# Forgetting-attention scores from split float32r operands, in a hybrid decoder block on one core

## The chip, the cores and the metric

The kernel runs on one core of one Trainium2 chip. Its metric is device time in microseconds (us), from the start to the end of one execution. TensorE (PE in the profile) multiplies, VectorE (DVE) and ScalarE (ACT) do elementwise work, GpSimd (POOL) and SyncE (SP) mostly issue DMAs.

## The reference, cut to what matters

A decoder block over 272 tokens (16 meta tokens and 256 of the input), width 2048: one large projection feeds a gated DeltaNet branch and a forgetting-attention branch of 16 heads, both are gated and merged, and an MLP follows. The change lies in the scores of the attention branch.

```python
q = heads(rms_norm(q.reshape(B, L, FOX_HEADS, FOX_DH), q_norm_g))   # 16 heads of 128
k = heads(rms_norm(k.reshape(B, L, FOX_HEADS, FOX_DH), k_norm_g))
...
s = jnp.einsum('bhqd,bhkd->bhqk', qs, k).astype(jnp.float32) * scale
s = s + cq[..., :, None] - c[..., None, :]
s = jnp.where(kpos[None, :] <= qpos[:, None], s, -jnp.inf)
p = jax.nn.softmax(s, axis=-1).astype(v.dtype)
return jnp.einsum('bhqk,bhkd->bhqd', p, v)
```

Only the 256 input tokens are kept as queries (two tiles of 128); the first tile sees 144 keys, the second 272.

## The kernel before, in words

Weights stream from HBM in blocks of 1 MB. SP issues the loads, and `split` (L126) turns each half block into a high and a low float32r part: ACT copies it to `wh`, DVE subtracts to get `wl`. The pool `wspl` keeps three such pairs. A gemm with stationary weights (`gemm_ws`, L156) takes 16 steps of contraction, so two blocks and four splits; each step has three products (L168, L169, L170) for each of two column groups, 96 in all, into two PSUM banks (`acc`). The pool `psA` has four such banks, so a gemm takes the banks of the gemm two before it, and can start only when these have been read.

The stage around the change is the value projection of the attention branch: eight gemms, one for a pair of heads, called V0 to V7 here (L950). After each, two heads are put on a task list, an even and an odd one. A head is a generator (`fox_head`, L885): after every step of a gemm each head on the list is advanced to its next `yield`, so heads are recorded between the steps of later gemms. V0 to V7 are followed by four gemms on `C_Z` columns (`gemm_ts`, L971), called Z0 to Z3, recorded after all heads have ended.

A head does this: DVE reads its bank and scales it to `vt` (L888), which frees the bank; POOL issues a DMA that copies it to `vb`. PE makes the scores (L894 to L897) from `qf` and `kf`, with a masking product in bfloat16 for each tile; DVE scales them to `tl` (L902), finds the maxima `nm`, ACT takes exponentials, DVE divides by the sum; POOL issues a DMA `tl` to `tb`. PE transposes `vb` ("v flips") and `tb` with a small tile `pm` ("p flips"), both on L94; the results are split into high and low (`vnh`, `vnl`, `pth`, `ptl`, and `ptm` for the meta tokens); L939 to L944 are the products of probabilities and values, and `ybh`, `ybl` the result.

All temporary tiles of a head come from pools with a fixed number of buffers in rotation: `t272` (129 to 272 elements a partition) has 12, `t512` has 4. Before the change a head takes four of `t272`: `vt`, `vb`, `vnh`, `vnl`. The order of instructions on each engine is set when the program is built: a scheduler orders them by its own estimates, within what the pools allow, and each engine then runs its row strictly in that order.

Of the kernel before, what the change touches and what calls it, by code (L numbers as in the profile page):

```python
# [9 lines left out]
F32R = mybir.dt.float32r  # L10
BF16 = mybir.dt.bfloat16
AF = mybir.ActivationFunctionType
ALU = mybir.AluOpType
AX = mybir.AxisListType

P = 128
# [3 lines left out]
T = NM + 256  # L20
# [13 lines left out]
def hybrid_block(ctx: ExitStack, tc: tile.TileContext, x, meta_tokens, mix_norm_g, w_in, conv_w, a_log,  # L34
# [23 lines left out]
    def tt(shape, name, dtype=F32):  # L58
        n = 1
        for d in shape[1:]:  # L60
            n *= d
        for size, tag in ((128, "t128"), (272, "t272"), (512, "t512")):
            if n <= size:
                return tmp.tile(shape, dtype, name=name, tag=tag, bufs=TMP_BUFS[tag])
        raise ValueError(n)

    def big_tile(shape, name, dtype=F32):
        return big.tile(shape, dtype, name=name, tag="big")
# [4 lines left out]
    def ps_tile():  # L73
        return psS.tile([P, 512], F32, name="ps", tag="ps")

    def acc_tile():
        return psA.tile([P, 512], F32, name="acc", tag="acc")

    act, dve, pe, pool = nc.scalar, nc.vector, nc.tensor, nc.gpsimd

    def acopy(out, in_, scale=1.0):
        act.activation(out=out, in_=in_, func=AF.Copy, scale=scale)  # L82

    def f(ap):
        return ap.bitcast(F32)
# [11 lines left out]
    def stack(dst, src, both):  # L97
        n = list(src.shape)
        one = 1 if both == (0, 2) else 2
        acopy(dst[..., both[0]:both[1] + 1:both[1] - both[0], :], src.unsqueeze(len(n) - 1).broadcast_to(n[:-1] + [2, n[-1]]))  # L100
        dve.tensor_tensor(out=dst[..., one, :], in0=src, in1=f(dst[..., 0, :]), op=ALU.subtract)
# [20 lines left out]
    def pause(n):  # L122
        for _ in range(n):
            yield
# [96 lines left out]
    with tc.high_priority():  # L221
# [3 lines left out]
        for i in range(4):  # L225
            s = slice(i * 512, (i + 1) * 512)
# [14 lines left out]
    identb = const.tile([P, P], BF16, name="identb")  # L241
# [3 lines left out]
    maskb = const.tile([P, P], BF16, name="maskb")  # L245
# [10 lines left out]
    ps = acc_tile()  # L256
# [570 lines left out]
    kf = big_tile([P, H, T], "kf")  # L827
# [56 lines left out]
    rng = (slice(0, 144), slice(144, 416))  # L884
    def fox_head(h, acc):  # L885
        qf, rq = QF[h], RQ[:, h, :]
# [3 lines left out]
        vb = bits(vt[:, NM:T], [P, 256], "vb")  # L890
        vs = tt([P, 3, NM], "vs", F32R)
        stack(vs, vt[:, 0:NM], (0, 2))
        ps = ps_tile()
        pe.matmul(ps[:, 0:144], qf[:, 0:P], kf[:, h, 0:144], start=True, stop=False)  # L894
        pe.matmul(ps[:, 16:144], identb, maskb, start=False, stop=True)
        pe.matmul(ps[:, 144:416], qf[:, P:256], kf[:, h, :], start=True, stop=False)  # L896
        pe.matmul(ps[:, 288:416], identb, maskb, start=False, stop=True)  # L897
        tl = tt([P, 416], "tl")
        nm = tt([P, 2], "nm")
        su = tt([P, 2], "su")  # L900
        for t in range(2):
            dve.scalar_tensor_tensor(out=tl[:, rng[t]], in0=ps[:, rng[t]], scalar=rq[:, t:t + 1],  # L902
                                     in1=NC[:, h, 0:144 + 128 * t], op0=ALU.mult, op1=ALU.add)
# [4 lines left out]
        ps = ps_tile()  # L908
# [18 lines left out]
        ps, ps2 = ps_tile(), ps_tile()  # L927
# [10 lines left out]
        ps = ps_tile()  # L938
# [10 lines left out]
    for hp in range(H // 2):  # L949
        accs = gemm_ws(win, C_FV + hp * 256, u, 0, T)  # L950
        for c in range(2):
            tasks.append(fox_head(2 * hp + c, accs[c]))
# [17 lines left out]
    for n in range(4):  # L970
        accs = gemm_ts(win, C_Z + n * 512, u_t(0), u_t(1), KT)  # L971
        yy = []
        for t in range(2):
# [4 lines left out]
            for i in range(4):  # L978
                h = 4 * n + i
# [5 lines left out]
        for i in range(2):  # L985
            ps = ps_tile()
# [192 lines left out]
```

## Time and profile before

| | |
|---|---|
| median of 3 runs | 1989.97 us (1988.95 to 1992.73) |
| the profiled execution | 1992.09 us, span 1990.3 us |
| PE, DVE, ACT, POOL busy | 1966.9, 1200.4, 1008.2, 115.1 us |
| mean granted TensorE clock | 0.997 |
| value stage with its heads | about 616 to 770 us |

Busy time of an engine is the union of its instructions. A matmul's row shows how long it lies in the pipeline; what it costs in a stream is the distance from its start to the next start. The share of an engine over the whole span says little on one stage, so the stage is read by itself.

### The profile page before, as it was taken

The numbers are of one execution on the slowest core, as the hardware profiler recorded it, in microseconds if no ns is written. First come the engines' busy times: TensorE is split into PE (matmuls) and PEld (weight loads), VectorE is DVE, ScalarE is ACT, GpSimd is POOL, SyncE is SP. The second block draws the span as 40 slices with busy tenths as digits, with TensorE's granted clock in tenths as the row PEclk, the third lists the DMA queues.
The fourth block names the chain that finished last, engine by engine and source line by source line (L and its number), as shares of the span: only waits on it lengthen the run. The fifth ranks groups of instructions, "written<-read, shape, count | busy, mean of one in ns | idle before, by whom it ended". The sixth has DMA issues, their size and how long they took to land.

```text
span 1990.3 us, 30185 instructions
## 1 busy us (share of the span) xinstructions
PE 1966.9 (99%) x11974; PEld 1735.0 (87%) x11974; DVE 1200.4 (60%) x2005; ACT 1008.2 (51%) x1797; POOL 115.1 (6%) x168
## 2 busy tenths in 40 slices
PE   8999999999999999999999999999999999999998
PEld 7898999999999998888888888888888888888886
DVE  5786846677546776644444555566655456665555
ACT  5644466556555555444444445555543345554444
POOL 0022100011131110000000000000000000000000
PEclk9999999999999999999999999999999999999999
DMA  6556766544566545656565666666655566666555
GB/s 201 171 162 204 217 179 205 165 140 141 182 210 198 165 165 200 203 190 201 190 201 190 201 243 212 199 188 188 188 191 193 197 194 186 188 186 212 196 197 176
DMA packets 283139, 378.77 MB, mean 190 GB/s; under 512 B 24163, under 2 KB 190406, under 8 KB 282470
## 3 DMA queue, kind: packets, MB, share of 16 engines
q1 hardware_dynamic: 275584, 353.65, 56.3%
q0 software_dynamic: 7200, 22.92, 3.5%
q8 instruction: 94, 1.54, 0.3%
q14 instruction: 47, 0.39, 0.1%
q10 hardware_dynamic: 214, 0.28, 0.0%
HBM read 351.63 MB, written 3.76 MB: 179 GB/s over the span
## 4 chain that ended last, share of the span: by engine, by line
PE 93%; issue 3%; DMA 2%; DVE 1%; ACT 0%; SPq 0%; POOL 0%; POOLq 0%; DVEq 0%; ACTq 0%
PE acc L165 15%; PE acc L183 15%; PE acc L185 15%; PE acc L184 15%; PE acc L170 14%; PE acc L168 7%; PE acc L169 7%; PE ps L94 1%; DVE wl L131 1%; DMA kb<-kT 1%; PE ps L552 0%; DMA rawS<-in_w_in_dram 0%; PE ps L896 0%; PE ps L628 0%; DMA dY<-I 0%
## 5 line engine op out<-in xcount | busy, mean ns | idle before, releaser
L131 DVE TENSOR_TENSOR wl<-raw,wh 128x1024 fp32r<-128x1024 f32 x644 | 787.7, 1224 | 635.1 <-ACT wh L82 631.8
L82 ACT ACTIVATE wh<-raw 128x1024 fp32r<-128x1024 f32 x644 | 682.1, 1060 | 751.8 <-PE acc L185 463.7
L170 PE MATMUL acc<-u,wl 128*128 128x272 f32 (+2 forms) x1536 | 440.5, 290 | 0.6 <-DVE wl L131 0.6
L168 PE MATMUL acc<-u,wh 128*128 128x272 f32 (+1 forms) x1280 | 373.0, 293 | 1.0 <-DVE ca L465 1.0
L169 PE MATMUL acc<-u,wh 128*128 128x272 f32 (+1 forms) x1280 | 371.8, 291 | 0.0
L165 PE MATMUL acc<-v,wh 128*128 128x512 f32 x1024 | 355.8, 396 | 0.0
L170 PEld LDWEIGHTS acc<-u,wl 128*128 128x128 f32 x1536 | 289.6, 189 | 3.2 <-DVE wl L131 1.2
L170 PE MATMUL acc<-v,wl 128*128 128x256 f32 x1024 | 279.3, 279 | 0.0
L168 PEld LDWEIGHTS acc<-u,wh 128*128 128x128 f32 x1280 | 241.6, 189 | 2.3 <-DVE ca L465 1.5
L169 PEld LDWEIGHTS acc<-u,wh 128*128 128x128 f32 x1280 | 243.0, 190 | 0.7 <-issue 0.2
L165 PEld LDWEIGHTS acc<-v,wh 128*128 128x128 f32 x1024 | 189.5, 188 | 42.8
L184 PE MATMUL acc<-wl,h1h 128*128 128x512 f32 x504 | 196.1, 389 | 0.0
L185 PE MATMUL acc<-wh,h1l 128*128 128x512 f32 x504 | 196.1, 389 | 0.0
L170 PEld LDWEIGHTS acc<-v,wl 128*128 128x128 f32 x1024 | 192.9, 188 | 3.5
L183 PE MATMUL acc<-wh,h1h 128*128 128x512 f32 x504 | 176.3, 389 | 0.0
L185 PE MATMUL acc<-wh,u 128*128 128x512 f32 x384 | 151.6, 395 | 0.0
L184 PE MATMUL acc<-wl,u 128*128 128x512 f32 x384 | 151.1, 394 | 0.0
L183 PE MATMUL acc<-wh,u 128*128 128x512 f32 x384 | 139.2, 396 | 0.0
L183 PEld LDWEIGHTS acc<-wh,h1h 128*128 128x128 f32 x504 | 94.6, 188 | 19.8
L185 PEld LDWEIGHTS acc<-wh,h1l 128*128 128x128 f32 x504 | 94.6, 188 | 19.6
L184 PEld LDWEIGHTS acc<-wl,h1h 128*128 128x128 f32 x504 | 94.6, 188 | 19.4
L165 PE MATMUL acc<-u,wh 128*128 128x512 f32 x256 | 89.5, 395 | 0.0
(378 smaller groups left out, 2387.8 us busy)
## 6 DMA issues: line engine op xcount, KB each, us to landing
raw<-in_w_in_dram SPq DMA_DIRECT2D x142, 1024.0 KB, 5.2
raw<-in_w_down_dram SPq DMA_DIRECT2D x66, 1024.0 KB, 5.2
raw<-in_w_up_dram SPq DMA_DIRECT2D x64, 1024.0 KB, 5.8
raw<-in_w_o_gdn_dram SPq DMA_DIRECT2D x16, 1024.0 KB, 5.2
raw<-in_w_o_fox_dram SPq DMA_DIRECT2D x16, 1024.0 KB, 5.4
raw<-in_w_out_dram SPq DMA_DIRECT2D x16, 1024.0 KB, 5.3
vb<-vt POOLq DMA_DIRECT2D x32, 128.0 KB, 2.2
tb<-tl POOLq DMA_DIRECT2D x16, 208.0 KB, 2.2
```

The source lines that it names most:

```text
L82: act.activation(out=out, in_=in_, func=AF.Copy, scale=scale)
L94: pe.transpose(out=out.bitcast(F32R), in_=in_, identity=identr)
L131: dve.tensor_tensor(out=wl, in0=raw, in1=f(wh), op=ALU.subtract)
L165: pe.matmul(accs[c][:, 0:2 * n].rearrange("p (a n) -> p a n", a=2), wh[:, s], m[kt // 8][:, kt % 8, :, n0:n1], start=(kt == 0), stop=False)
L168: pe.matmul(o, wh[:, s], part(m, kt, 0, n0, n1), start=(kt == 0), stop=False)
L169: pe.matmul(o, wh[:, s], part(m, kt, 1, n0, n1), start=False, stop=False)
L170: pe.matmul(o, wl[:, s], part(m, kt, 0, n0, n1), start=False, stop=(kt == KT - 1))
L183: pe.matmul(accs[t], a, wh, start=(kt == 0), stop=False)
L184: pe.matmul(accs[t], a, wl, start=False, stop=False)
L185: pe.matmul(accs[t], b, wh, start=False, stop=(kt == nkt - 1 - (last if t else 0)))
```

## The change

The queries and keys of a head are split when the head begins: ACT copies them to `qh` and `kh` in float32r, DVE subtracts to get `ql` and `kl`. After a pause of four steps the scores are made of three float32r products for each tile (high by high, high by low, low by high) in place of one float32 product, and the masking product follows as before. The four new tiles come from the pool `t272`, whose 12 buffers stay.

```diff
-        ps = ps_tile()
-        pe.matmul(ps[:, 0:144], qf[:, 0:P], kf[:, h, 0:144], start=True, stop=False)
-        pe.matmul(ps[:, 16:144], identb, maskb, start=False, stop=True)
-        pe.matmul(ps[:, 144:416], qf[:, P:256], kf[:, h, :], start=True, stop=False)
-        pe.matmul(ps[:, 288:416], identb, maskb, start=False, stop=True)
+        qh, ql = [tt([P, 256], name, F32R) for name in ("qh", "ql")]
+        kh, kl = [tt([P, T], name, F32R) for name in ("kh", "kl")]
+        acopy(qh, qf)
+        acopy(kh, kf[:, h, :])
+        dve.tensor_tensor(out=ql, in0=qf, in1=f(qh), op=ALU.subtract)
+        dve.tensor_tensor(out=kl, in0=kf[:, h, :], in1=f(kh), op=ALU.subtract)
+        yield from pause(4)
+        ps = ps_tile()
+        for t in range(2):
+            s, n = slice(t * P, (t + 1) * P), 144 + 128 * t
+            pe.matmul(ps[:, rng[t]], qh[:, s], kh[:, 0:n], start=True, stop=False)
+            pe.matmul(ps[:, rng[t]], qh[:, s], kl[:, 0:n], start=False, stop=False)
+            pe.matmul(ps[:, rng[t]], ql[:, s], kh[:, 0:n], start=False, stop=False)
+            pe.matmul(ps[:, 16 + 272 * t:144 + 272 * t], identb, maskb, start=False, stop=True)
```

The change also gives the engines another order. On PE, before, at the p flips of an even head in V3 (`acc_8264` and `acc_8265` are V3's banks):

```order
L94 MATMUL ps_8190<-identr_94,tb_8130 128x128 x3
L94 MATMUL ps_8191<-identr_94,pm_8132 48x128 x2
L168 MATMUL acc_8265<-u0_140,wh_8268 128x272
L169 MATMUL acc_8265<-u0_140,wh_8268 128x272
L170 MATMUL acc_8265<-u0_140,wl_8269 128x272
...
L939 MATMUL ps_8218<-ptm0_4209,vnm0_4207 128x256
```

and now, on PE, at the p flips of the even head that stands at the end of V3 (`acc_8548` is the first bank of V4, L948 to L953 are the old L939 to L944):

```order
L94 MATMUL ps_8266<-identr_94,tb_8209 128x128 x3
L94 MATMUL ps_8267<-identr_94,pm_8211 48x128 x2
L948 MATMUL ps_8298<-ptm0_4209,vnm0_4207 128x256
L951 MATMUL ps_8298<-pth_8273,vnh_8182 128x256
L94 MATMUL ps_8309<-identr_94,vb_8187 128x128 x2
L94 MATMUL ps_8309<-identr_94,vs_8189 48x128
L952 MATMUL ps_8298<-ptl_8274,vnh_8182 128x256
L953 MATMUL ps_8298<-pth_8273,vnl_8183 128x256
L951 MATMUL ps_8298<-pth_8273,vnh_8182 128x128
L952 MATMUL ps_8298<-ptl_8274,vnh_8182 128x128
L953 MATMUL ps_8298<-pth_8273,vnl_8183 128x128
L168 MATMUL acc_8548<-u0_140,wh_8552 128x272
```

Before, 24 products of the gemm stand between the p flips and the first product that needs their results; now none does, and the next gemm begins behind the head's products.

On DVE, before, at the place where the bank of the third pair's even head is read (`acc_8024`, V2; `wl_8390` and `wl_8449` are the third and fourth split of V3):

```order
L131 TENSOR_TENSOR wl_8390<-raw_8387,wh_8389 128x1024
L919 RECIPROCAL su_8171<-su_8171 128x2
L936 TENSOR_TENSOR ptl_8198<-ps_8190,pth_8197 128x384
L921 TENSOR_SCALAR tl_8169<-tl_8169,su_8171 128x144
L921 TENSOR_SCALAR tl_8169<-tl_8169,su_8171 128x272
L131 TENSOR_TENSOR wl_8449<-raw_8387,wh_8448 128x1024
L101 TENSOR_TENSOR pm_8249<-tl_8169,pm_8249 128x2x16
L917 TENSOR_TENSOR vnl_8234<-ps_8229,vnh_8233 128x256
L888 TENSOR_TENSOR vt_8278<-acc_8024,RU_139 128x272
```

and now (`acc_8020`, V2; `wl_8686` is the third split of V4, whose first product takes this very bank):

```order
L911 SCALAR_TENSOR_TENSOR tl_8245<-ps_8236,RQ_178,NC_6173 128x144
L911 SCALAR_TENSOR_TENSOR tl_8245<-ps_8236,RQ_178,NC_6173 128x272
L131 TENSOR_TENSOR wl_8686<-raw_8683,wh_8685 128x1024
L913 TENSOR_REDUCE nm_8246<-tl_8245 128x1 x2
L944 CAST ptm0_4209<-ps_8267 48x256
L945 TENSOR_TENSOR ptl_8274<-ps_8266,pth_8273 128x384
L928 RECIPROCAL su_8247<-su_8247 128x2
L930 TENSOR_SCALAR tl_8245<-tl_8245,su_8247 128x144
L930 TENSOR_SCALAR tl_8245<-tl_8245,su_8247 128x272
L926 TENSOR_TENSOR vnl_8314<-ps_8309,vnh_8313 128x256
L888 TENSOR_TENSOR vt_8318<-acc_8020,RU_139 128x272
```

The read of V2's bank moved from behind the fourth split of V3 to behind the third split of V4. In both rows it stands right behind the `vnl` of the odd head before it, which is the tile ahead of it in the pool.

## Rows read from the trace of the kernel before

**Rows 1.** The page, busy time by engine.
```profile
PE 1966.9 (99%) x11974; PEld 1735.0 (87%) x11974; DVE 1200.4 (60%) x2005; ACT 1008.2 (51%) x1797; POOL 115.1 (6%) x168
```
**Rows 2.** Windows: one pair of heads; length, busy by engine, clock, DMA.
```profile
684.76:701.48 16.72, 16.72 (x141) 16.45 (x140) 12.74 (x33) 9.21 (x24) 2.14 (x4) 1.00 0.55 168
```
**Rows 3.** Timeline of PE: start, length, what; one head's scores.
```profile
623.69 0.47 PE L894 MATMUL ps<-kf,qf 128*128 128x144 f32 x2
...
624.05 0.68 PE L896 MATMUL ps<-kf,qf 128*128 128x272 f32 x2
...
624.80 0.29 PE L170 MATMUL acc<-u,wl 128*128 128x272 f32 x1
624.93 0.29 PE L168 MATMUL acc<-u,wh 128*128 128x272 f32 x1
```
**Rows 4.** Timeline of PE: float32r products of a head, 128 columns wide.
```profile
635.31 0.22 PE L942 MATMUL ps<-pth,vnh 128*128 128x128 f32 x1
635.37 0.28 PE L943 MATMUL ps<-ptl,vnh 128*128 128x128 f32 x1
635.48 0.27 PE L944 MATMUL ps<-pth,vnl 128*128 128x128 f32 x1
```
**Rows 5.** Timeline of PE: p flips of a head, and L939.
```profile
671.80 0.37 PE L94 MATMUL ps<-identr,tb 128*128 128x128 f32 x3
672.01 0.28 PE L94 MATMUL ps<-identr,pm 128*48 128x128 f32 x2
...
675.21 0.28 PE L939 MATMUL ps<-ptm,vnm 128*128 128x256 f32 x1
```
**Rows 6.** Timeline of DVE, 668 to 679 us.
```profile
668.80 0.42 DVE L917 TENSOR_TENSOR vnl<-ps,vnh 128x256 fp32r<-128x256 f32 x1
669.14 0.43 DVE L888 TENSOR_TENSOR vt<-acc,RU 128x272 f32<-128x272 f32 x1
669.69 0.78 DVE L902 SCALAR_TENSOR_TENSOR tl<-ps,RQ,NC 128x144 f32<-128x144 f32 x2
...
672.34 0.42 DVE L935 CAST ptm<-ps 48x256 fp32r<-48x256 f32 x1 [0.55 <-PE ps L94]
672.68 1.21 DVE L131 TENSOR_TENSOR wl<-raw,wh 128x1024 fp32r<-128x1024 f32 x1
673.81 0.15 DVE L919 RECIPROCAL su<-su 128x2 f32<-128x2 f32 x1
673.88 0.53 DVE L936 TENSOR_TENSOR ptl<-ps,pth 128x384 fp32r<-128x384 f32 x1
674.34 0.55 DVE L921 TENSOR_SCALAR tl<-tl,su 128x144 f32<-128x144 f32 x2
...
679.02 0.64 DVE L904 TENSOR_REDUCE nm<-tl 128x1 f32<-128x144 f32 x2
```
**Rows 7.** Timeline of ACT, the same stretch.
```profile
668.23 0.38 ACT L82 ACTIVATE vnh<-ps 128x256 fp32r<-128x256 f32 x1 [0.60 <-PE ps L94]
...
673.29 0.47 ACT L82 ACTIVATE pth<-ps 128x384 fp32r<-128x384 f32 x1
```
**Rows 8.** DMA issues of the stage: count, KB, median us to landing.
```profile
tb<-tl POOLq DMA_DIRECT2D x16, 208.0 KB, 2.2
```
**Rows 9.** Groups by line and form, 616 to 772 us: mean ns after the comma.
```profile
L976 ACT ACT_TABLE_LOAD x1 | 1.3, 1283 | 0.0
L976 ACT ACTIVATE sg<-acc,rs 128x512 f32<-128x512 f32 x2 | 1.3, 682 | 0.0
L977 DVE SCALAR_TENSOR_TENSOR sg<-acc,rs,sg 128x512 f32<-128x512 f32 x2 | 1.4, 747 | 0.7 <-ACT sg L976 0.7
```
**Rows 10.** Windows around two pauses of PE: columns as in rows 2.
```profile
18.00:20.00 2.00, 0.77 (x7) 0.55 (x5) 0.14 (x1) 0.22 (x1) 0.89 (x1) 1.00 0.54 63
...
22.00:24.40 2.40, 2.40 (x12) 2.10 (x11) 2.40 (x3) 0.62 (x2) 0.00 (x0) 0.50 0.89 273
...
259.00:261.00 2.00, 0.71 (x8) 0.59 (x8) 0.88 (x1) 0.00 (x0) 0.00 (x0) 1.00 1.47 141
```

## The prediction

> **What bounds the kernel now.** I read the busy times first: TensorE is busy 1966.9 of 1990.3 us, VectorE 60% and ScalarE 51% [rows 1]. Those are averages, so I then read the stage that is changed by itself. A pair of heads takes 16.72 us there, and TensorE is busy for all of it, VectorE for 12.74, ScalarE for 9.21 [rows 2]. So TensorE's stream is the path. A product taken out of it is worth its distance to the next start, and work on the other engines costs nothing as long as TensorE never waits for it. What keeps TensorE from waiting is the order: the p flips of a head start at 671.80, and the first product that needs their results starts at 675.21 [rows 5]. In between VectorE and ScalarE make `ptm` (ends 672.76), `pth` (673.76) and `ptl` (674.41) [rows 6, 7], and TensorE runs 24 products of the gemm meanwhile. The banks are read early too: an even head's `vt` ends at 669.57, the first split of the gemm that takes this bank is only written from 672.68 to 673.89 [rows 6]. That is 4.3 us in hand.
>
> **The products.** One head's scores take from 623.69 to the second gemm product at 624.80, less one gemm slot of 0.13: 0.98 us with both masks and the hitch behind the last one [rows 3]. The new products are float32r, of the kind that the gemms and L942 to L944 have. A 272-column one costs a slot of 0.13 [rows 3], three cost 0.38. A 128-column one costs 0.06 or 0.11 [rows 4]; I take 0.11 for the 144-column ones, as most stand before a product with new weights: 0.33. A mask costs the rest of what is measured; with the hitch before float32r weights I put it at 0.115, so 0.23. The sum is 0.94, a saving of 0.05 a head and 0.8 us for 16 heads. The bounds: with 0.06 for each narrow product and each mask and 0.12 for the wide ones it is 0.66, a saving of 5 us in all; with 0.12, 0.13 and 0.12 it is 0.99, nothing saved.
>
> The trace shows a float32 product as two records, and the pair of 272 columns lies 0.68 us in the pipeline [rows 3]. The Trainium skill, "FP8 and Floating Point Precision", section "Matmul Precision", counts true FP32 as four passes through the array, so that three single passes would save a quarter of the products' time; of about 0.8 us that is an estimate of 0.2 a head and 3 us in all. It lies within the bounds above, which rest on rows, and I keep 0.8.
>
> **The splits.** `qh` and `kh` are two copies on ScalarE, `ql` and `kl` two subtractions on VectorE. None is in the trace; the nearest rows are `vnh` with 0.38 and `vnl` with 0.42 [rows 6, 7]. A pair of heads so adds 1.7 us to VectorE and 1.5 to ScalarE: 14.4 and 10.7 of 16.72. Neither becomes the bound by its load, so as load they cost nothing. The change adds no DMA; POOL's two for each head and SP's loads stay in their turn. If the cover were gone they would cost 1.7 us a pair.
>
> **The buffers and the order.** This is where I expect the time to go. A head now takes eight tiles of `t272` in place of four, a pair sixteen, and the pool has twelve. Counted in the order in which they are taken, `kh` of an even head gets the buffer of the even `vnl` before it, which is read until that head's last product. So the scores of one pair cannot start before the products of the last are done; before the change, heads overlapped. The order shown with the change says what the scheduler made of it. The read of a bank (`vt`) stands behind the odd head's `vnl` as before, but that is now reached behind the third split of the very gemm that needs the bank. And on TensorE nothing of a gemm is left between the p flips and that gemm's first product: the gemm before has ended, the next one has no bank. What was hidden under 24 products now stands in the open once for each gemm.
>
> I work out one such place, the start of V4, counting from the end of the p flips. The odd head's scores reach VectorE 0.3 us before that. Then its row runs: `tl` 0.78, a weight split 1.21, two maxima 0.64, `ptm` 0.42, `ptl` 0.53, `su` 0.15, the division 0.55, `vnl` 0.42, `vt` 0.43 [rows 6]. The sum is 5.13 - 0.3; neighbours on VectorE overlap by some 0.1 each, but `su` waits for ScalarE's exponentials a little, so I take 4.5 us until TensorE may start V4. In this time it has its own work: L948 and the first L951 at 0.12, three v flips at some 0.2 [rows 5], the five other products at some 0.5 [rows 4], 0.94 together. That leaves 3.6 us of waiting. The other places have the same chain with fewer links. V7 has all of them: 3.7. At V5 and at Z0 `su` and the division come later: 2.7 each. At V6 the odd head's scores stand behind the flips and fill part: 2.1. At V3 and Z1 some gemm products are left: 0.5 each. At Z2 the chain is another one: the banks of Z0 are read only when the last head's `pth` (0.47) is done, and then a table load (1.28), a sigmoid (0.68) and a multiplication (0.75) follow [rows 7, 9]; with 0.3 until `pth` starts that is 3.5, less 0.8 of products, 2.7. V0 to V2 start as before. The sum is 3.6 + 3.7 + 2 x 2.7 + 2.1 + 2 x 0.5 + 2.7 = 18.5 us. From below: at each of the six larger places at least `pth`, `vnh`, `vnl`, `vt` (0.47 + 0.38 + 0.42 + 0.43 = 1.70) must run in turn, less 0.94 of TensorE's work: 0.8 each, 5 us. From above: half as much again, where links wait for each other in the engines' rows, 28 us.
>
> The Trainium skill, "Perfetto Trace Analysis", section "Identifying Performance Opportunities", says that the same gap repeating on the engine that should be saturated can mean that no buffer is free for the next tile. The trace of before has no such gap in this stage; the forecast is that it appears.
>
> **The sum.** +18.5 - 0.8 = +17.7 us. The profiled execution of before took 1992.09 us, its span being 1990.3; it lies 2.1 above the median of the runs. On the profiled execution that gives 2010, on the median of 1989.97 some 2007, which is my number.
>
> **The rivals.**
> *The banks come in time.* If a pair's loop from `vt` to the next `vt` fits into 16.7 us of TensorE's work, no gemm waits, and only the products' saving is left: 1989, between 1985 and 1990, so not slower. For it speaks that the loads fit (14.4 of 16.7) and that 4.3 us are in hand today. It decides at the place where `vt` of an even head stands against the third split of the gemm that takes its bank; that the split stands ahead of `vt` in the row speaks against it, since the split's buffer is free only when the gemm before has ended. Chance 0.13; in 0.03 of it the saving is over 4 us.
> *The clock falls in the pauses.* The granted clock went to the lower level, 1.2 GHz, once after TensorE had been busy only 0.77 of 2 us and had then waited 1.9 [rows 10], and was still there when it was busy again: 2.4 us from 22.00 show 0.50. Another pause, 0.71 busy of 2 us at 259, left it at 1.00, which is 2.4 GHz. At the new waits TensorE is busy 0.94 of 4.5 us. Those 2.4 us at half speed cost 1.2 us, so I put a fall at 1.2 to 1.7; at six places that is 7 to 10 more, 2014 to 2017. Chance 0.13. The Trainium skill, "TensorE: Matmul & The Clock Gate", warns in "Why this matters for your kernels" that pauses between bursts of matmuls put the clock back; the two pauses show that it may or may not.
> *The loop waits for the DMA.* The p flips need `tb`, which lands 2.2 us after its issue [rows 8], behind the exponentials and the division. By my count it comes 0.3 to 3.4 us ahead of the flips. If splits that wait for TensorE hold ScalarE and VectorE up, TensorE waits here too: 1.5 us at 12 heads is 18 more, 2025. Chance 0.07.
>
> **How the numbers follow.** The forecast, waits at gemm starts without the other two, has 0.67. Its own range goes from the least waits with the greatest saving (5 - 5, so 1990) to the greatest waits with none (1990 + 28 = 2018); the lower end needs both extremes at once, so I take 1995. The clock case lies inside up to 2019. Left out are the rival of 0.13 below and most of the 0.07 above: the range is 1995 to 2019. A measurement can tell about 0.2%, 4 us, from no change. Faster by more: 0.03. Within it: 0.10 of the rival and 0.02 for a forecast that comes out very small, 0.12. Slower: 0.85.
>
> **What would show it.** In the profile of the changed kernel TensorE should be idle some 15 to 20 us more between 616 and 810, waiting for `vt`, `ptl`, `pth` and `sg` at seven or eight gemm starts, 2 to 4 us each, and a pair of heads from V3 on should take 18.5 to 20.5 us in place of 16.72. The score products of a head should take 0.94 us from first to last when they stand together. I am wrong if TensorE's stretch is unbroken there, if the waits lie at the scores (for `kl` or `kh`) or at the flips (for `tb`), or if the windows show a clock below 1.00.

## The result, and the profile after

The changed kernel takes 2020.12 us (median of 4 runs, 2018.36 to 2020.67), the kernel before beside it 1991.1. The ratio is 1.0144 with a 95% interval of 1.0132 to 1.0156: slower by 1.4%, some 29 us. The forecast was 2007 in a range of 1995 to 2019 (the sum itself gives 2007.7). The direction and the waits were right, the sum was short by what the clock took.

The page of the changed kernel, busy time by engine, answers to [rows 1]:

```profile
PE 1981.9 (98%) x12006; PEld 1749.2 (87%) x12006; DVE 1212.1 (60%) x2037; ACT 1018.4 (50%) x1829; POOL 115.2 (6%) x168
```

TensorE has 15 us more of busy time with 32 more records. At 0.13 us each [rows 3] these are 4 us, so most of it must be slower work, not more of it. What TensorE waited for from 616 to 830 us (engine, tile and line, what ended the wait; us in total, times, longest), where the same view of the kernel before has no line:

```profile
PE ps L948 <- DVE ptm L944: 6.0, 5, 2.0
PE ps L952 <- DVE ptl L945: 4.8, 4, 1.6
PE acc L168 <- DVE vt L888: 1.8, 4, 0.9
PE acc L183 <- DVE vt L888: 0.9, 2, 0.7
```

Three more lines of that view hold 1.5 us: 0.6 for `sg`, 0.6 for `tb` and 0.3 for `pth`. One of the places, the start of V5, in the timeline of TensorE (start, length, what, idle before it):

```profile
680.03 0.43 PE L94 MATMUL ps<-identr,tb 128*128 128x128 f32 x3
680.30 0.29 PE L94 MATMUL ps<-identr,pm 128*48 128x128 f32 x2
681.42 0.38 PE L948 MATMUL ps<-ptm,vnm 128*128 128x256 f32 x1 [0.83 <-DVE ptm L944]
...
681.76 0.29 PE L94 MATMUL ps<-identr,vb 128*128 128x128 f32 x2
683.23 0.39 PE L952 MATMUL ps<-ptl,vnh 128*128 128x256 f32 x1 [1.11 <-DVE ptl L945]
...
684.25 0.39 PE L168 MATMUL acc<-u,wh 128*128 128x272 f32 x1 [0.23 <-DVE vt L888]
...
685.31 0.43 PE L168 MATMUL acc<-u,wh 128*128 128x272 f32 x1
685.54 0.43 PE L169 MATMUL acc<-u,wh 128*128 128x272 f32 x1
```

In [rows 5] 24 gemm products, about 3 us, stand between the p flips and the first product that needs their result; here nothing does, and TensorE stands still three times. The windows of the stage show the rest (length, busy by engine, then the granted clock, as in [rows 2]):

```profile
640.00:660.90 20.90, 18.44 (x154) 17.79 (x152) 14.92 (x37) 11.52 (x30) 1.61 (x3) 1.00 0.57 175
660.90:667.70 6.80, 6.24 (x29) 6.05 (x29) 2.82 (x10) 1.88 (x7) 1.61 (x3) 0.50 0.22 78
...
684.80:688.30 3.50, 3.50 (x18) 3.50 (x17) 1.72 (x7) 0.52 (x3) 1.01 (x2) 0.51 0.28 98
...
705.30:708.70 3.40, 3.40 (x18) 3.40 (x17) 2.04 (x9) 1.06 (x6) 0.83 (x2) 0.50 0.11 39
...
725.80:732.60 6.80, 6.14 (x27) 6.14 (x27) 2.31 (x8) 1.21 (x5) 1.60 (x3) 0.50 0.20 70
732.60:807.70 75.10, 70.25 (x413) 59.92 (x412) 51.85 (x114) 41.46 (x93) 5.35 (x10) 1.00 0.49 165
807.70:811.10 3.40, 2.91 (x7) 2.34 (x8) 3.40 (x11) 0.50 (x2) 0.00 (x0) 0.50 0.00 1
```

Five times, each time in or behind the waits at a gemm's start, the granted clock is 0.50, the level of 1.2 GHz in place of 2.4. The last two products of the timeline above lie in the second of these stretches: their starts are 0.23 us apart, in place of 0.13 [rows 3]. Together the stretches are 23.9 us. If half of that time is lost, it is 12 us on top of the waits; without the 2 us in them in which TensorE waits, and at 0.23 against 0.13, it is about 10. The kernel before has no such stretch between 62 us and its end.

### The profile page after: what moved, and what is told of

It is laid out like the page before. It is cut to its first block, busy times and chain, and to the rows that moved or that the text cites. A ratio compares the mean times of both kernels' runs of the same rounds, so it can differ in the third digit from the quotient of the medians.

```text
span 2018.2 us, 30356 instructions
## 1 busy us (share of the span) xinstructions
PE 1981.9 (98%) x12006; PEld 1749.2 (87%) x12006; DVE 1212.1 (60%) x2037; ACT 1018.4 (50%) x1829; POOL 115.2 (6%) x168
## 4 chain that ended last, share of the span: by engine, by line
PE 91%; issue 3%; DMA 2%; DVE 2%; ACT 0%; SPq 0%; POOL 0%; POOLq 0%; DVEq 0%; ACTq 0%
PE acc L183 14%; PE acc L185 14%; PE acc L184 14%; PE acc L170 14%; PE acc L165 14%; PE acc L168 7%; PE acc L169 7%; PE ps L94 1%; DMA kb<-kT 1%; DVE wl L131 1%; PE ps L628 0%; PE ps L552 0%; DMA rawS<-in_w_in_dram 0%; DMA dY<-I 0%; DMA raw<-in_w_in_dram 0%
## 5 line engine op out<-in xcount | busy, mean ns | idle before, releaser
L168 PE MATMUL acc<-u,wh 128*128 128x272 f32 (+1 forms) x1280 | 378.6, 297 | 2.9 <-DVE vt L888 1.8
L169 PE MATMUL acc<-u,wh 128*128 128x272 f32 (+1 forms) x1280 | 375.6, 294 | 0.0
L170 PEld LDWEIGHTS acc<-u,wl 128*128 128x128 f32 x1536 | 293.9, 192 | 1.5 <-issue 0.2
L168 PEld LDWEIGHTS acc<-u,wh 128*128 128x128 f32 x1280 | 246.3, 193 | 5.0 <-DVE vt L888 2.5
L169 PEld LDWEIGHTS acc<-u,wh 128*128 128x128 f32 x1280 | 247.6, 193 | 0.3 <-issue 0.2
```

Of the source, the lines that this page charges most:

```text
L168: pe.matmul(o, wh[:, s], part(m, kt, 0, n0, n1), start=(kt == 0), stop=False)
L169: pe.matmul(o, wh[:, s], part(m, kt, 1, n0, n1), start=False, stop=False)
L170: pe.matmul(o, wl[:, s], part(m, kt, 0, n0, n1), start=False, stop=(kt == KT - 1))
```

## How the runs are counted

Three things are counted in each trace below. *Gaps* are TensorE's between 560 and 840 us: from the end of one product to the start of the next, plus the 0.16 us by which neighbours in a stream overlap, where that is over 0.26 us in all. *Low* is the time at the 1.2 GHz level after the first 100 us and before the end of the program. *Last head* is when the product of `vnm` and `ptm` (L939 before) of head 15 starts. The median of the kernel before was 1989.9 to 1992.0 us beside the runs; each ratio is to the one beside it. The sum column is 1990, plus the gaps beyond the 0.3 us of before, plus half of *low*, the larger of the two prices above. *Gaps*, *low* and *last head* are read from one profiled execution of each kernel, the medians from 4 runs or more.

| kernel | median, us | ratio, 95% interval | gaps | low | sum | last head |
|---|---|---|---|---|---|---|
| before | 1990 | | 0.3 | 0 | 1990 | 767 |
| changed | 2020.1 | 1.0132 to 1.0156 | 18.3 | 23.9 | 2020 | 805 |
| e1 splits in rooms | 2004.1 | 1.0047 to 1.0075 | 10.2 | 3.4 | 2002 | 793 |
| e2 e1, old products | 2006.8 | 1.0059 to 1.0084 | 11.7 | 13.7 | 2008 | 797 |
| e3 changed, old products | 1998.4 | 1.0021 to 1.0046 | 6.5 | 0 | 1996 | 788 |
| e4 changed, waits filled | 2010.5 | 1.0079 to 1.0106 | 7.3 | 0 | 2009 | 797 |
| e5 e1, vt in a room | 2004.4 | 1.0051 to 1.0077 | 7.4 | 13.7 | 2004 | 790 |
| e6 before, vt in a room | 1991.7 | 0.9997 to 1.0015 | 0 | 0 | 1990 | 764 |
| e7 before, pause | 1995.7 | 1.0015 to 1.0040 | 4.3 | 6.8 | 1997 | 788 |
| e8 changed, no pause | 2024.6 | 1.0154 to 1.0185 | 19.9 | 27.3 | 2023 | 809 |
| e9 e5, no pause | 2000.3 | 1.0035 to 1.0063 | 7.6 | 6.8 | 2001 | 787 |
| e10 e1, no pause | 2000.0 | 1.0038 to 1.0063 | 6.4 | 6.8 | 1999 | 785 |
| e11 e9, old products | 1991.6 | 0.9999 to 1.0017 | 1.9 | 0 | 1992 | 780 |
| e12 e3, splits held | 2006.0 | 1.0058 to 1.0085 | 9.7 | 6.8 | 2003 | 789 |
| e13 e9, splits made ahead | 2001.1 | 1.0035 to 1.0063 | 7.5 | 10.2 | 2002 | 786 |
| e14 e1, first heads on time | 2001.3 | 1.0037 to 1.0068 | 7.9 | 3.4 | 1999 | 790 |
| e15 e14, vt in a room | 1999.5 | 1.0040 to 1.0065 | 6.1 | 10.2 | 2001 | 784 |
| e16 e15, no pause | 1991.4 | 0.9996 to 1.0014 | 0.3 | 0 | 1990 | 778 |
| e17 e13, first heads on time | 1990.9 | 0.9997 to 1.0014 | 0.3 | 0 | 1990 | 779 |

For e4 the sum has 11.9 us more, its 99 added products at the 0.12 us between their starts. The sum meets every median within 3.2 us, with the old products and with the new. So to within these 3 us the time of each kernel is gaps and clock; how the scores are multiplied does not show at that size.

## Experiments: splits out of the shared buffers, and the clock

**e1: splits in rooms.** The four split tiles leave `t272`; they lie in rows of `ybh` that are not written yet and, from head 8, in rows of `NC` that are no longer read.

```diff
-        qh, ql = [tt([P, 256], name, F32R) for name in ("qh", "ql")]
-        kh, kl = [tt([P, T], name, F32R) for name in ("kh", "kl")]
+        room = ybh.rearrange("p h t -> p (h t)") if h < 8 else NC.rearrange("p h t -> p (h t)").bitcast(F32R)
+        c = (1984 if h < 8 else 0) + 1056 * (h % 2)
+        qh, ql, kh, kl = [room[:, c + a:c + b] for a, b in ((0, 256), (256, 512), (512, 784), (784, 1056))]
```

> The changed kernel with qh, ql, kh and kl moved out of the 12 shared buffers of t272: they lie in rows of ybh that are not yet written (heads 0 to 7) and in rows of NC that are no longer read (heads 8 to 15), two sets in turn. Same instructions, same products. Theory (buffers, then clock): the waits of TensorE in the value stage (18.6 us counted in the gaps) go, and with them the five stretches at the 1.2 GHz level in that stage (23.9 us of them, about 11 us lost); what is left is the saving by the products, 0.05 to 0.1 us a head: 1988 to 1990 us, level with the kernel before or up to 0.15% faster. Rival (load): the two splits of a head (two copies on ScalarE, two subtractions on VectorE) make VectorE late wherever the tiles lie; then most of the 18.6 us of gaps stay and the time is 2010 us or more. Rival (clock by itself): the clock falls because the products are float32r now, whatever the waits; then some 11 us stay, about 2000 us.

2004.1 us: none of the three. Four of the five clock falls and 16 us are gone, but 10.2 us of gaps stay, and they stand elsewhere: five of 1.31 to 1.44 us at the start of a gemm, for `vt`, and smaller ones. Two things were wrong with the theory. `vt` itself takes its buffer from `t272`, one that a `vnl` of the pair before holds until its last product, so that pool can be short without the splits too. And the rooms had a fault of their own, seen later (e14).

**e2: e1 with the float32 products of before.**

```diff
-            pe.matmul(ps[:, rng[t]], qh[:, s], kh[:, 0:n], start=True, stop=False)
...
+        pe.matmul(ps[:, 0:144], qf[:, 0:P], kf[:, h, 0:144], start=True, stop=False)
...
+        pe.matmul(ps[:, 144:416], qf[:, P:256], kf[:, h, :], start=True, stop=False)
...
```

> As the run before, but the scores are the two float32 products of before; the four split tiles are computed and not used. It measures the load of the splits alone, and against the run before the price of the products. Theory (buffers): the splits are hidden, 1990 us, no gap of 0.3 us or more in the value stage; the run with the new products is 1 to 2 us faster than this one. Rival (load): 2000 us or more.

2006.8, another miss: with nobody on TensorE reading the splits, the time is no better than e1. The scheduler gave TensorE another order, and the largest waits are now two for `tb`, 6.3 us in all. The comparison that was to price the products compares two orders instead.

**e3: the changed kernel with the float32 products**, the splits still in `t272`, computed and not read on TensorE (the edit of e2 alone).

> The changed kernel with the float32 products of before: the four split tiles are taken from the 12 shared buffers as in the changed kernel, computed, and not read by TensorE. Theory (buffers): the ring of 12 buffers is the same, so most of the waits and clock falls are the same; the time is 2015 to 2024 us. The buffers of the splits come free a little earlier here, since nobody on TensorE reads them. Rival (products): the new products hold the buffers or slow the engine; then this kernel is at 1990 to 1995 us.

1998.4, between the two ranges. The pool is the same, and three quarters of the loss are gone. TensorE's waits in it, from 616 to 830 us:

```profile
PE acc L168 <- DVE vt L888: 4.0, 3, 1.4
PE acc L183 <- DVE vt L888: 1.3, 1, 1.3
```

So the number of tiles is not the whole of it. How long they are held may count as well, since here VectorE is the last to use them; e12 tests that.

**e4: the waits filled.** The order and the waits of the changed kernel stay as nearly as they can; extra products stand where TensorE waited longest.

```diff
+    fills = {"vnm": {2: 12, 4: 6, 8: 15, 10: 6, 15: 4}, "ptl": {4: 8, 6: 12, 10: 8, 15: 7}, "end": {2: 4, 8: 6, 15: 5}}
+    def fill(where, h, ps, m):
+        for _ in range(fills[where].get(h, 0)):
+            pe.matmul(ps[:, 256:512], m[:, 0:P], m[:, 0:256], start=(where != "ptl"), stop=(where != "ptl"))
...
+        fill("vnm", h, ps, pth)
         pe.matmul(ps[:, 0:256], vnm, ptm, start=True, stop=False)
```

> The changed kernel with extra products on TensorE, 99 of 128x256 on pth into columns of ps that nobody reads, set where TensorE waited most: ahead of the product of vnm and ptm (heads 2, 4, 8, 10, 15), ahead of the first product of ptl (4, 6, 10, 15) and behind the last one (2, 8, 15). At 0.11 us each they are 10.9 us of work inside 16 us of waits, so they should cost little time themselves. Theory (the clock falls because the engine stands still): the stretches at the 1.2 GHz level in the value stage are gone or fewer, and up to 11 us come back: 2008 to 2013 us although the work is more. Rival (the waits alone cost the 29 us, the clock falls on its own): the falls stay where they were and the time is 2020 us or up to 10 us more.

2010.5 us, in the range of the theory: 99 products more, and 9.6 us faster. The gaps that are left and the products in them are 7.3 + 11.9 = 19.2 us, as much as the 18.3 us of gaps before. What went is the lower clock. The windows of this kernel, over stretches in which the changed kernel was at 0.50:

```profile
660.90:667.70 6.80, 6.72 (x57) 6.53 (x56) 3.48 (x12) 2.04 (x7) 1.60 (x3) 1.00 0.20 70
...
684.80:705.30 20.50, 20.28 (x171) 19.88 (x169) 15.60 (x40) 10.47 (x29) 2.14 (x4) 1.00 0.44 138
...
807.70:811.10 3.40, 3.40 (x20) 2.83 (x19) 3.40 (x7) 2.21 (x3) 0.00 (x0) 1.00 0.40 77
```

This settles the clock: these falls come because TensorE stands still, and they cost about 10 us of the 29. The Trainium skill, "TensorE: Matmul & The Clock Gate", section "Why this matters for your kernels", warns of pauses between bursts of matmuls. In kind these two kernels agree with it; the pauses that it names are longer than any here, where the longest single wait was 2.0 us, so on the size the measurement decides.

## Experiments: the parts one at a time

**e5: e1 with `vt` out of the pool too**, in the row of `kf` of four heads before.

```diff
-        vt = tt([P, T], "vt")
+        vt = tt([P, T], "vt") if h < 4 else kf[:, h - 4, :]
```

> The run with the splits in rooms of their own (2004.1 us) still waits 1.43 us at the start of six gemms for vt. The buffer of vt is one that a vnh or vnl of the pair before holds until its last product, in the kernel before too. Here vt of heads 4 to 15 lies in a row of kf that is no longer read, so t272 serves six tiles a pair of heads instead of eight (before) and sixteen (changed kernel). Theory (buffers): with that no tile waits for a buffer of the pair before, the gaps of 1.43 us and the fall of the clock at 748 us go, and the time is 1988 to 1992 us, level with the kernel before. Rival (load or order): VectorE and ScalarE are late at the end of a pair because of the two copies and two subtractions; vt then still ends last and the time stays at 2000 to 2004 us.

2004.4, as the rival said, but not by its cause. From 645 to 782 us there is not one gap. But for a wait of 1.0 us at 644 us and a fall of the clock at 411 us, outside the stage, the loss moved to the end: the last heads stand alone there, with 3.56 us of waiting for `tb`, three waits of 0.6 to 0.8, and 10.2 us at the lower clock.

**e6: that move of `vt` in the kernel before**, as a control.

> The kernel before with vt of heads 4 to 15 in dead rows of kf, nothing else: a control for the run above. In the kernel before no wait over 0.2 us stands in the value stage, so there is nothing to win: 1989 to 1991.5 us. If it is faster by 2 us or more, the 12 buffers already cost the kernel before something; if it is slower, the place itself costs and the run above has to be read against this one.

1991.7, no difference: the twelve buffers cost the kernel before nothing.

**e7: the pause alone**, in the kernel before.

```diff
         stack(vs, vt[:, 0:NM], (0, 2))
+        yield from pause(4)
         ps = ps_tile()
```

> The kernel before with one part of the change alone: the pause of four steps ahead of the scores. No splits, old products. Theory (buffers): 1989 to 1993 us, since no tile is added; a head only takes four steps longer. Rival (the pause is the cause: a head that is longer holds its vnh, vnl and vt longer and comes into the way of the next pair): 2000 us or more.

1995.7, between the two: the pause by itself costs about 5 us. The last head comes at 788 us, not 767, and three gemms wait 1.2 to 1.4 us for `vt`; its 6.8 us at the lower clock lie at 262 us, ahead of the stage. The prediction gave the pause no term at all.

**e8: the changed kernel without the pause.**

```diff
-        yield from pause(4)
         ps = ps_tile()
         for t in range(2):
```

> The changed kernel without the pause of four steps ahead of the scores; splits in the shared t272, new products. Theory (buffers): the split tiles are given back four steps earlier, but sixteen tiles a pair still share 12 buffers: waits of 10 to 18 us and clock falls remain, 2008 to 2022 us. Rival (the pause is the cause): 1992 to 1998 us.

2024.6, a little over the expected range and 4.5 us more than with it. So taking the pause out does not help while the splits stand in the shared buffers.

**e9, e10, e11: rooms and no pause.** e9 is e5, e10 is e1, without the pause; e11 is e9 with the float32 products.

> The run with rooms of their own for the splits and for vt, now also without the pause of four steps ahead of the scores. In the run with that pause the value stage has no gap after its first pair, but the heads are some 15 to 23 us later than in the kernel before (last product of vnm and ptm at 790 us instead of 767), and the last head, with no gemm left beside it, costs 6.7 us of gaps and 10.2 us at the lower clock. Theory (length of a head): without the pause the last head comes at 765 to 775 us again, both losses go, and the time is 1988 to 1992 us. Rival (the splits themselves make a head late, pause or not): last head at 785 us or later, 1998 to 2004 us.

> As the run beside it, but vt stays in t272, so that t272 serves eight tiles a pair as in the kernel before. Theory (buffers and length of a head): a head is a little longer than before by its splits, so vt gets its buffer a little later; gaps at the start of gemms of 0 to 1 us each, 1990 to 1998 us, between the run beside it and the one with splits in rooms and the pause (2004 us). Rival (the buffer of vt is the whole cause there): 2000 to 2004 us, as with the pause.

> As the first run of these three, with the float32 products of before in place of the six float32r products; the splits are computed and not used. It prices the products where nothing waits: from the slots read in the traces, 0.88 us a head against 0.985 us, this run should be 1.7 us slower than the first (1 to 3 us). Rival (the products save nothing, since the engine waits elsewhere): the same time within 0.5 us.

2000.3, 2000.0 and 1991.6. e9 and e10 came out in the ranges of their rivals, e11 in neither. e10 keeps two waits for `vt`, 3.7 us in all. e9 has the gaps of e5 at the end of the stage again. And e11, with the products that were to be slower, is 9 us faster than e9: a price of the products of the wrong sign and of five times the size. The timelines show why. In e9 the first score waits for its splits, and these come late; ScalarE's first copy in e1, and in the changed kernel:

```profile
627.34 0.42 ACT L82 ACTIVATE ybh<-qf 128x256 fp32r<-128x256 f32 x1
```
```profile
617.98 0.40 ACT L82 ACTIVATE qh<-qf 128x256 fp32r<-128x256 f32 x1
```

`ybh` takes the buffer that `RK` leaves, so nothing can be written there before the last keys are scaled with `RK`; that ends at 627.6 us in e9, and the first copy starts at 627.62. In e11 the scores don't read the splits, and the first head is on time: its product of `vnm` and `ptm` starts at 633 us, in e9 at 645. Of these 12 us 7 are left at the last head: before, that product comes every 8.4 us up to the end of V7, as often as half a gemm of 8.36 us [rows 2], so a head has little time in hand. So e1, e5, e9 and e10 carry a loss that is the experiment's own. The scores of e2 don't read the splits, and its first head is on time (638 us); what its two waits for `tb` come from stays open.

**e12: the splits held.** e3, with two products of 128x16 behind the scores that read the four tiles on TensorE.

```diff
+        pe.matmul(ps[:, 416:432], qh[:, 0:P], kl[:, 0:16], start=True, stop=True)
+        pe.matmul(ps[:, 416:432], ql[:, 0:P], kh[:, 0:16], start=True, stop=True)
```

> The changed kernel with the float32 products of before; the four split tiles stand in the 12 shared buffers and are held until TensorE reads them at the place of the new products: two products of 128x16 into columns of ps that nobody reads stand in the place. It differs from the run with old products and splits that nobody on TensorE reads (1998.4 us, 6.5 us of gaps, no fall of the clock) only by that. Theory (the buffers are short because the products hold them until TensorE has read them): gaps of 12 to 18 us and two or more falls of the clock come back, 2008 to 2020 us. Rival (what the changed kernel loses beyond 1998 us is that its scores wait for the splits, not that buffers are held): 1996 to 2002 us.

2006.0, between the ranges: 7.6 us over e3, with a fall of the clock, and the waits at L948 and L952 are back:

```profile
PE acc L168 <- DVE vt L888: 3.3, 3, 1.1
PE ps L952 <- DVE ptl L945: 1.2, 2, 1.0
PE ps L948 <- DVE ptm L944: 1.1, 2, 0.6
```

Holding the tiles costs some. The other 14 us lie between e12 and the changed kernel, whose scores wait for the splits; the order differs too, and which of the two it is no run shows.

**e13: splits made ahead**, behind the softmax of the head before, in the rooms of e9. `split_head` holds the four instructions and the rooms of e1.

```diff
                            accum_out=su[:, t:t + 1])
+        if h + 1 < H:
+            split_head(h + 1)
         yield from pause(4)
```

> The new products with splits in rooms of their own and vt in dead rows of kf, no pause, and the splits of a head made half a gemm earlier, behind the softmax of the head ahead of it, so that no score waits for them. Counted in the gaps and clock falls, all kernels run so far are 1960 us of products plus their gaps plus half of the time at the lower clock, within 2 us. Theory (gaps, clock, and no saving by the products): with the chain of a head as short as in the kernel before, the last head comes at 765 to 782 us, gaps in the stage are under 3 us, and the time is 1989 to 1993 us; a version that beats the kernel before by more than 1 us does not come out of this change. Rival (the new products save the 0.1 us a head that their slots show): 1987 to 1988.5 us.

2001.1, in neither range: the late start again, with that product of the first head at 644 us.

## Experiments: a ladder with the first heads on time

In these four, heads 0 and 1 take their splits from `t272` as in the changed kernel, and heads 2 to 15 have the rooms. e14 is e1 with that, e15 e5, e16 e9, e17 e13.

```diff
+        if h < 2:
+            qh, ql = [tt([P, 256], name, F32R) for name in ("qh", "ql")]
+            kh, kl = [tt([P, T], name, F32R) for name in ("kh", "kl")]
+        else:
...
```

> The first run with rooms (e1) made cleaner. There the rooms of the first heads lie in ybh, whose buffer is the one that RK leaves, so the first splits could not be written before the last keys were scaled with RK, at 626 us instead of 618, and every head was late from then on. Here heads 0 and 1 take their splits from t272 as the changed kernel does, heads 2 to 15 have the rooms; vt stays in t272, the pause stays. Theory (buffers and the delay of the first head): the first product of vnm and ptm at 640 us as in the changed kernel, the waits for vt at the gemms' starts as in e1 or a little shorter, the last head at 783 to 790 us; 1996 to 2003 us. Rival (the shared buffers are no part of the loss beyond what e1 shows, and neither is the late start): 2003 to 2006 us, as e1.

> As the run beside it with vt of heads 4 to 15 in dead rows of kf: no shared buffer is short any more, the pause of four steps stays. Against e5 (2004.4 us) only the start of the first two heads differs. Theory: the first head no longer starts late, so the last one comes at 776 to 784 us instead of 790, while the second gemm of the next stage still runs beside it; the gaps at the end shrink from 6.7 us to 0 to 4 us: 1990 to 1997 us. Rival (a head is too long for its 8.4 us in any case, by two subtractions on VectorE): last head at 790 us, 2002 to 2005 us.

> As the run beside it, without the pause of four steps. Against e9 (2000.3 us) only the start of the first two heads differs. Theory: last head at 772 to 780 us, gaps of 0 to 3 us in the stage, 1988.5 to 1993 us. Rival (a head too long in any case): 1998 to 2001 us.

> As e13 (2001.1 us, splits made behind the softmax of the head ahead), with the splits of heads 0 and 1 in t272, so that the first head starts on time. Theory: last head at 768 to 778 us, gaps under 2 us, no fall of the clock in the stage, 1988 to 1991.5 us; the new products then cost or save under 1 us against the kernel before. Rival (a head too long in any case): 1998 to 2002 us.

Here "on time" means as in the changed kernel: that product of the first head starts at 638 to 640 us. e14, e16 and e17 came out in the ranges of their theories; e15 lies between its two. From the changed kernel to e16 they differ by one step each, and can be read as a ladder:

- Changed kernel to e14, only the splits of heads 2 to 15 out of `t272`: 2020.1 to 2001.3, and in ratios to the kernel before, 1.0144 to 1.0053. The splits in the shared buffers are 18 of the 29 us.
- e14 to e15, `vt` out as well: 2001.3 to 1999.5, with the same ratio of 1.0053. It moves the waits more than it ends them.
- e15 to e16, the pause out: 1999.5 to 1991.4, 8 us.
- e16 to before: 1.4 us, interval -0.04% to +0.14%. Splits and products together cost nothing that can be told.

The size of a step depends on what was taken out before it: the pause alone, taken from the changed kernel, made it 4.5 us slower (e8), and here, as the last step, it gives 8 us back.

In e14 the chain at a gemm's start is short and always the same. VectorE at one of them:

```profile
695.84 1.23 DVE L131 TENSOR_TENSOR wl<-raw,wh 128x1024 fp32r<-128x1024 f32 x1 [1.31 <-ACT wh L82]
696.99 0.42 DVE L961 TENSOR_TENSOR ybl<-ps,ybh 128x256 fp32r<-128x256 f32 x1
697.32 0.41 DVE L931 TENSOR_TENSOR vnl<-ps,vnh 128x256 fp32r<-128x256 f32 x1
697.65 0.43 DVE L888 TENSOR_TENSOR vt<-acc,RU 128x272 f32<-128x272 f32 x1
```

and TensorE, which has ended the scores and needs that bank:

```profile
696.48 0.23 PE L911 MATMUL ps<-maskb,identb 128*128 128x128 bf16 x1
698.14 0.39 PE L168 MATMUL acc<-u,wh 128*128 128x272 f32 x1 [1.43 <-DVE vt L888]
```

In e15 no gemm waits up to 776 us. There the heads end too late, and the last one runs with no gemm beside it. TensorE at that place, and the windows before it and from it on:

```profile
778.55 0.22 PE L94 MATMUL ps<-identr,vs 128*48 128x128 f32 x1
782.25 0.59 PE L94 MATMUL ps<-identr,tb 128*128 128x128 f32 x3 [3.48 <-DMA tb<-tl]
782.65 0.41 PE L94 MATMUL ps<-identr,pm 128*48 128x128 f32 x2
783.66 0.55 PE L953 MATMUL ps<-ptm,vnm 128*128 128x256 f32 x1 [0.60 <-DVE ptm L949]
```
```profile
616.00:776.00 160.00, 160.00 (x1177) 150.28 (x1176) 123.92 (x292) 94.95 (x230) 16.64 (x32) 1.00 0.55 175
...
782.20:792.40 10.20, 8.72 (x27) 6.98 (x28) 6.03 (x17) 4.68 (x7) 0.00 (x0) 0.50 0.14 53
```

A pause of four steps moves the last head from 778 us (e16) to 784 us. Six microseconds there cost 6 us of gaps and 10.2 us at half speed. Without it, in e16, TensorE is busy throughout:

```profile
616.00:640.00 24.00, 24.00 (x201) 23.82 (x200) 19.13 (x44) 14.71 (x36) 2.23 (x5) 1.00 0.64 190
640.00:700.00 60.00, 60.00 (x508) 59.64 (x507) 51.11 (x129) 37.02 (x96) 7.98 (x15) 1.00 0.54 170
700.00:760.00 60.00, 60.00 (x394) 53.71 (x393) 45.73 (x106) 35.91 (x86) 6.38 (x12) 1.00 0.51 171
760.00:830.00 70.00, 69.88 (x343) 57.44 (x342) 49.28 (x85) 37.52 (x52) 0.54 (x1) 1.00 0.61 204
```

It is the whole change but for the pause and the place of the tiles, and it is level with the kernel before, not ahead of it; so is e17. No version came out of this that beats the kernel before.

The cause is settled as far as these edits go: tiles held in a pool that has no room, and a head made longer. What is not settled is how much of each wait is the pool itself and how much the order that the scheduler makes of it. Each edit gave the engines another order, and none was run in the order of another.

## Why the prediction was right or wrong

*The waits: right.* 18.5 us were forecast; the gaps grew by 18.0. By place, forecast and then measured: V3 0.5 and 0.3, V4 3.6 and 3.3, V5 2.7 and 2.7, V6 2.1 and 1.8, V7 3.7 and 3.5, Z0 2.7 and 2.7, Z1 0.5 and 0.8, Z2 2.7 and 3.1. V0 to V2 start as before. Reading VectorE's new row link by link, with durations from [rows 6], was enough for that. What ended them was `ptm`, `ptl` and `vt`, as the chain said; none lay at the scores, and one of 0.6 us at `tb`. At two places the size is partly luck: at V4 that wait for `tb`, which the chain does not hold, is a quarter of the gap. At Z2 the forecast had `pth` and `sg`; the trace has `ptm` and `ptl` too, and a weight split of 1.23 us stands ahead of `ptl` in VectorE's row. The Trainium skill, "Perfetto Trace Analysis", section "Identifying Performance Opportunities", has the repeating gap for a want of free buffers; the trace agrees, with gaps at eight gemm starts, and e14 takes most of them away by moving tiles.

*The clock: the step that failed.* The prediction held the falls as a rival beside the forecast, with a chance of 0.13 and 7 to 10 us, and added nothing for them to the sum; a clock below 1.00 was one of its own signs of being wrong, and that sign came. A pair of heads took 20.3 to 22.3 us from gemm start to gemm start, where 18.5 to 20.5 was forecast. The falls are not another way that the time could go, they are a consequence of the waits: whoever forecasts eight pauses must say in the same sum what the clock does in them. The size was short as well. It was taken from one stretch of 2.4 us at 0.50 in [rows 10], 1.2 to 1.7 us a fall. The trace of before holds more: that fall lasted 3.4 us, and a second one stands at 58.5 us, behind small products (L414 to L423) and without a wait:

```profile
21.00:24.40 3.40, 2.87 (x14) 2.40 (x13) 3.40 (x6) 1.62 (x3) 0.00 (x0) 0.50 0.75 207
58.50:61.90 3.40, 3.40 (x17) 3.08 (x17) 0.85 (x6) 2.38 (x6) 0.00 (x0) 0.50 0.00 0
```

In the changed kernel there were five falls of 23.9 us in all, 10 to 12 us lost, 2.0 to 2.4 each, because two of them lasted 6.8 us. With 18.5 and 10 to 12, less 0.8, the same working gives 2018 to 2020 on the median that was used, which lies 1.1 us below the one beside the run.

*The products: not shown.* A saving of 0.05 us a head was forecast. In e16, in a stream, a head's scores take 0.89 us from the first slot to the last mask's; in the kernel before 0.90 to 0.95 where all records are there and nothing stands between. 16 times the difference is at most 1 us, and the medians don't show it: e16, and e11 with the old products, are at 1991.4 and 1991.6. The saving of 3 us that the estimate from the pass counts would give is not there.

*The splits as load: right.* From 616 to 830 us of e16 VectorE is busy 165.2 us and ScalarE 125.2, in the kernel before 153.3 and 114.0; 12 and 11 us more, where 13.6 and 12 were forecast for eight pairs, and no gap comes of it. The windows, before and then e16:

```profile
616.00:830.00 214.00, 213.88 (x1415) 193.10 (x1415) 153.28 (x329) 113.99 (x236) 18.24 (x34) 1.00 0.56 183
616.00:830.00 214.00, 213.88 (x1438) 194.61 (x1437) 165.24 (x362) 125.15 (x269) 17.14 (x33) 1.00 0.57 184
```

*The buffers: right in the place, too simple in the cause.* The prediction laid all waits on sixteen tiles in twelve buffers. e14 shows that this is the larger part. But e3, with the same sixteen tiles released early, loses 7 us and not 29, and e7, with no tile more, loses 5. The pause of four steps was left without a term.

*The rivals.* That the banks come in time is what e16 and e17 do and the changed kernel does not. The wait for the DMA was one of 0.6 us in the changed kernel, but became the last head's in e5, e9, e13 and e15.

## What to carry to other kernels

A forecast of pauses on TensorE is not complete without the clock: here each microsecond of waiting cost more than half of another one, and 99 useless products in the waits made the kernel 9.6 us faster. Before adding tiles to a pool that rotates, ask how long each is held and by whom, and whether the chain that runs beside the gemms still ends before the last of them; a chain with little time in hand makes up only part of a late start. And an experiment that moves tiles can bring a wait of its own, so look where the first instruction starts before reading its time.

## What the runs showed of the hardware that was not expected

Equal pauses did not have equal effects on the clock. In the changed kernel the waits at the start of V5 and at Z0 are the same three, 0.83, 1.11 and 0.23 us; behind the first the clock is at 0.50 from 684.8 to 688.3 us, behind the second it stays at 1.00, as the window from 732.6 on shows. The three at Z0:

```profile
745.90 0.39 PE L948 MATMUL ps<-ptm,vnm 128*128 128x256 f32 x1 [0.83 <-DVE ptm L944]
...
747.71 0.39 PE L952 MATMUL ps<-ptl,vnh 128*128 128x256 f32 x1 [1.11 <-DVE ptl L945]
...
748.73 0.50 PE L183 MATMUL acc<-wh,u 128*128 128x512 f32 x1 [0.23 <-DVE vt L888]
```

In e14 five waits of 1.39 to 1.44 us at gemm starts brought one fall. The pause at 260 us, a wait for the DMA that writes `I` [rows 10], lies in a stage that none of these edits touches, and yet its length differs from trace to trace. In the kernel before, e16, e2 and e7:

```profile
260.37 0.31 PE L552 MATMUL ps<-I,XT 32*32 32x32 f32 x4 [1.29 <-DMA I<-dY]
257.94 0.31 PE L552 MATMUL ps<-I,XT 32*32 32x32 f32 x4 [1.49 <-DMA I<-dY]
260.11 0.31 PE L552 MATMUL ps<-I,XT 32*32 32x32 f32 x4 [1.56 <-DMA I<-dY]
260.53 0.31 PE L552 MATMUL ps<-I,XT 32*32 32x32 f32 x4 [1.82 <-DMA I<-dY]
```

Behind the first two the clock stays at 1.00; behind the other two it is at 0.50 for 6.8 us, in e2 here:

```profile
261.30:268.10 6.80, 6.80 (x84) 6.51 (x83) 3.78 (x8) 3.47 (x7) 0.00 (x0) 0.50 0.95 305
```

So whether a pause brings a fall can't be told from its own row alone; and some 3 us of a kernel's time come and go with one.
